# One hybrid block on one core: the opening in another order, and the plain gate and up blocks exchanged on the second half of the tokens

## The chip, the cores and the metric

The kernel runs on one core of a Trainium2 chip. The time is device microseconds of one launch; of several runs the median is shown. TensorE (PE in the profile) does the matrix products and the transposes, VectorE (DVE) and ScalarE (ACT) the elementwise work, SyncE (SP) issues most of the transfers, GpSimd (POOL) little. Each engine works through its own queue in order; semaphores hold an instruction until what it reads has been written, and until the room that it writes is free.

## The reference

One layer of a decoder block on 1024 tokens of width 1024, in float32:

```
h = rms_norm(x, attn_norm_w)
q, k, v, u, g = split(h @ w_in)            # 1024, 1024, 1024, 2048, 2048 columns
y_a = diff_attention(norm(q), norm(k), v) normed per head @ w_proj_attn
y_b = silu(layer_norm(conv31(u_a * sigmoid(u_b)))) @ w_proj_conv
x = x + (sigmoid(g_a) * y_a + sigmoid(g_b) * y_b) @ w_out
h = rms_norm(x, ffn_norm_w)
x = x + (silu(h @ W_gate) * (h @ W_up)) @ w_down          # FF = 2816 = 22 blocks of 128
```

## The kernel before, in words

**Products in three parts.** Every operand of a large product is split into a high part (a cast by ScalarE, `split_hi`, L120) and a low part (operand minus high part, VectorE, `split_lo`, L125). A product is three matmuls for each 128 of the contraction: high by high, high by low, low by high. So a tile is of use to TensorE only when ScalarE and then VectorE have been over it; a weight tile is 128x1024.

**The opening (`opening`, L817).** Tokens go in eight tiles of 128. For each: load (`xload`, two halves of 256 KB), sum of squares (`squares_of`, ScalarE), reciprocal root (`roots`: one VectorE instruction `v`, a root on ScalarE, five small VectorE instructions), scale by root and norm weight (`scale_x`, VectorE, two halves, reads `wb`, the norm weight broadcast to 128 partitions, called `anw_b` in the profile), transpose by TensorE in two halves (`turn_x`), and high and low part (`hi_x`, `lo_x`) into `hT_hi` and `hT_lo`. Beside it the first half of V is worked out, token tile by token tile: four weight pairs of 512 KB (`v_load`), cast by `w_hi(0..3)` and `w_lo(0..3)`, and 24 matmuls for each tile (`v_terms`). `TERMS` is the usual order, 8 steps of the contraction by three terms; in the first tile `halves` puts all terms with the high weights first. `v_out` splits the result and stores it. `w_hi(4)`, `w_lo(4)`, `w_hi(5)`, `w_lo(5)` are the two weight tiles of the first U block, loaded by `u_load` into the room of the first two V pairs (`wraw`, two buffers). After three V tiles the U block runs on token tiles 0 to 3 (`u_half`, L966) with the norm of tiles 4 to 7 between its matmuls.

**What sets the order.** A planner orders the program's instructions for each engine by a simulated time line. Inside `in_order(...)` (L199) the order of the code is kept on the engines named: in the three blocks of the opening TensorE, ScalarE, VectorE and SP. Each block ends with a `yield`, after which the loop at L996 may add taps of the convolution, once there are any. So in the opening the order in the code is the order on the engines, and what stands behind a waiting instruction waits too.

**The gate and up part.** Of the 22 blocks the first two (0 and 1) are done plainly, each on two halves of the tokens: `gate(f, sb, w)` is one GEMM of 24 matmuls and a silu, `up(f, sb, w, sg)` one GEMM and a product, stored to DRAM. `W[0]` and `W[1]` are the gate and up weights of block 0, `W[2]` and `W[3]` those of block 1. `W[0]` to `W[2]` lie in the three rotating buffers `whi`/`wlo`; `W[3]` (`fourth`, L538) lies in the room of the tile T4h. The second token half needs the norm of tiles 4 to 7 (`rest_of_rows`). The other 20 blocks go through a seven-product scheme (`pair`, L1661) which needs sums and differences of the token quarters: `differences()` (L1546) works out four differences per token tile in `xa` (16 VectorE operations) and splits them into T1 to T4 (16 casts, 16 low parts). It also needs sums of weight quarters, `s12` and `s34` in `prepare` (L1617; `s` in the profile), which lie in room that `xa` gives up. `prepare` takes the rotating buffers in turn: A11 and A12 come into the buffer of `W[0]`, the split of `s12` into that of `W[1]`, the split of `s34` into that of `W[2]`. `pair` starts with A11, A12, then S2 by T2 and S1 by T1.

Of the kernel before, what the change touches and what calls it, by code (L numbers as in the profile page):

```python
# [57 lines left out]
def kernel(  # L58
# [27 lines left out]
    nc = tc.nc  # L86
# [52 lines left out]
    def pg():  # L139
        npg[0] += 1  # L140
        p_, tag = pgs[npg[0] % len(pgs)]
        return p_.tile([P, 512], F32, tag=tag, name=nm("pg"))
# [48 lines left out]
    xload(0, 0)  # L191
    xload(0, 1, nc.scalar)
    for g in range(2):
        nc.scalar.dma_start(
            wb[:, 512 * g : 512 * (g + 1)], attn_norm_w[:, 512 * g : 512 * (g + 1)].to_broadcast([P, 512])
        )

# [505 lines left out]
    TERMS = [(k, a_, b_) for k in range(NKT) for a_, b_ in ((0, 0), (0, 1), (1, 0))]  # L703
# [113 lines left out]
    def opening():  # L817
# [11 lines left out]
        def u_load(z):  # L829
            c0 = (U0 + D, U0)[z]  # L830
            nc.sync.dma_start(
                uraw[z][:].rearrange("p (k c) -> p k c", c=P),
                win[:, c0 : c0 + P].rearrange("(k p) c -> p k c", p=P),
            )
# [8 lines left out]
        def w_hi(k):  # L843
            split_hi(tiles[k][0][:], raw6[k][:])

        def w_lo(k):
            split_lo(tiles[k][1][:], raw6[k][:], tiles[k][0][:])
# [3 lines left out]
        E_ = mybir.EngineType  # L851
        R, PT_ = {}, {}

        def turn_x(i, g):
            PT_[i, g] = x_turn(i, g)

        def hi_x(i, g):
            x_place(i, g, PT_[i, g], False)

        def lo_x(i, g):  # L860
            x_place(i, g, PT_[i, g], True)

        def squares_of(i, n):
            ss = sm.tile([P, 2], F32, tag="ss", name=nm("ss"))
            for e in range(n):
                x_squares(i + e, ss[:, e : e + 1])
            return ss

        def roots(i, n, ss):
            r = rstd_of(ss[:, :n], n, 1.0 / D)  # L870
            for e in range(n):
                R[i + e] = r[:, e : e + 1]

        def scale_x(i):
            for g in range(2):
                x_scale(i, R[i], g)

        with in_order(E_.PE, E_.Activation, E_.DVE, E_.SP):
            v_load(0)
            v_load(1)  # L880
            x_load(1)
            v_load(2)
            v_load(3)
            for i in range(2, NT):
                x_load(i)
            R[0] = x_first()
            scale_x(0)
            w_hi(0)
            turn_x(0, 0)
            hi_x(0, 0)  # L890
            turn_x(0, 1)
            lo_x(0, 0)
            w_hi(1)
            hi_x(0, 1)
            lo_x(0, 1)
            w_lo(0)
            ss = squares_of(1, 1)
            w_lo(1)
            u_load(0)
            u_load(1)  # L900
            roots(1, 1, ss)
            w_hi(2)
            scale_x(1)
            w_hi(3)
            w_lo(2)
            w_lo(3)
            o = pg()
            halves = [[(k, a_, 0) for a_ in range(2) for k in range(4 * g, 4 * g + 4)] for g in range(2)]
            v_terms(o, halves[0], w, 0, True, False)
            v_terms(o, halves[1], w, 0, False, False)  # L910
            v_terms(o, [(k, 0, 1) for k in range(4)], w, 0, False, False)
            turn_x(1, 0)
            hi_x(1, 0)
            lo_x(1, 0)
            turn_x(1, 1)
            ss = squares_of(2, 2)
            hi_x(1, 1)
            lo_x(1, 1)
            v_terms(o, [(k, 0, 1) for k in range(4, 8)], w, 0, False, True)
            roots(2, 2, ss)  # L920
            scale_x(2)
            v_out(0, 0, o)
        yield
        with in_order(E_.PE, E_.Activation, E_.DVE, E_.SP):
            o = pg()
            v_terms(o, TERMS[:12], w, 1, True, False)
            for g in range(2):
                turn_x(2, g)
                hi_x(2, g)
                lo_x(2, g)  # L930
            scale_x(3)
            w_hi(4)
            ss = squares_of(4, 2)
            v_terms(o, TERMS[12:], w, 1, False, True)
            roots(4, 2, ss)
            v_out(0, 1, o)
        yield
        with in_order(E_.PE, E_.Activation, E_.DVE, E_.SP):
            o = pg()
            v_terms(o, TERMS[:12], w, 2, True, False)  # L940
            for g in range(2):
                turn_x(3, g)
                hi_x(3, g)
                lo_x(3, g)
            w_lo(4)
            scale_x(4)
            w_hi(5)
            w_lo(5)
            ss = squares_of(6, 2)
            v_terms(o, TERMS[12:], w, 2, False, True)  # L950
            roots(6, 2, ss)
            scale_x(5)
            v_out(0, 2, o)
        yield

# [8 lines left out]
        sg = {}  # L964
# [581 lines left out]
    def differences():  # L1546
# [11 lines left out]
        for z in (2, 1, 3, 4):  # L1558
            for i in range(4):
# [2 lines left out]
                split_hi(T[z][0][:, :, ts], src)  # L1562
                split_lo(T[z][1][:, :, ts], src, T[z][0][:, :, ts])

    sg = gate(0, 1, W[0])
    up(0, 1, W[1], sg)
    differences()
    sg = gate(1, 1, W[2])
    up(1, 1, W[3], sg)
    n2_ctx.close()  # L1570
    xp_ctx.close()

# [229 lines left out]
```

## Time and profile before

| | before |
|---|---|
| three runs | 1762.86, 1764.28, 1766.6 us |
| median | 1764.28 us |
| the profiled execution, its own time | 1765.22 us |
| its span | 1763.4 us |
| TensorE busy | 1737.2 us (99%) |
| VectorE busy | 1272.2 us (72%) |
| ScalarE busy | 799.0 us (45%) |

The profile is of one execution. Times in its rows are microseconds from the start of the span. A row of the timeline gives start, length, engine, line of the program, operation, what is written and read, and, where the engine was idle before, for how long and who released it. In such names `px` is a transposed half token tile, `vwh`/`vwl` the V weights, `whi`/`wlo` other weights, `acc` and `pg` accumulators, `h_hi`/`h_lo` the second norm's result. Records of a matmul overlap: each lasts 0.39 us while the next starts 0.23 us behind it.

### The profile page before, as it was taken

How to read it: one execution, taken by the hardware profiler on the slowest of the kernel's cores; microseconds unless marked ns; L12 is line 12 of the kernel's file. 1: busy time of each engine (PE TensorE's matmuls, PEld its weight loads, DVE VectorE, ACT ScalarE, POOL GpSimd, SP SyncE). 2: the span in 40 equal slices, each digit the busy share in tenths (PEclk: the TensorE clock that was granted, in tenths of full speed). 3: DMA queues.
4: the chain of work that ended last, by engine and by line, in shares of the span. 5: the costliest groups of instructions: out<-in, count | busy, mean ns of one | idle time of the engine just before them, and what ended most of it. 6: DMA issues, size and time to landing. Idle time of an engine off the chain costs nothing.

```text
span 1763.4 us, 24974 instructions
## 1 busy us (share of the span) xinstructions
PE 1737.2 (99%) x8983; PEld 1481.3 (84%) x8983; DVE 1272.2 (72%) x2166; ACT 799.0 (45%) x1876; POOL 19.6 (1%) x92
## 2 busy tenths in 40 slices
PE   6999999999999999999999999999999999999999
PEld 5778898998989998988887888878888888888887
DVE  6598888998888888985877425867667666665544
ACT  5221141557767776764456213633333333333333
POOL 0000000000000000000000000000000000000000
PEclk9999999999999999999999999999999999999999
DMA  6337333235443344353863544224544544697663
GB/s 235 108 126 233 127 111 114 69 106 137 111 148 102 88 115 146 99 157 127 289 217 120 162 167 144 90 93 153 171 157 151 175 157 144 204 361 247 215 215 131
DMA packets 249814, 274.22 MB, mean 156 GB/s; under 512 B 16362, under 2 KB 165907, under 8 KB 249691
## 3 DMA queue, kind: packets, MB, share of 16 engines
q1 hardware_dynamic: 247834, 266.42, 46.9%
q0 software_dynamic: 1280, 4.91, 0.9%
q8 instruction: 70, 1.15, 0.3%
q10 hardware_dynamic: 576, 1.31, 0.2%
q14 instruction: 54, 0.43, 0.1%
HBM read 176.07 MB, written 78.16 MB: 144 GB/s over the span
## 4 chain that ended last, share of the span: by engine, by line
PE 90%; DMA 3%; DVE 3%; ACT 2%; issue 1%; SPq 0%; ACTq 0%; DVEq 0%
PE acc L1656 21%; PE pg L153 12%; PE pg L154 12%; PE pg L155 12%; PE acc L497 12%; PE pg L691 4%; PE sc L1056 2%; PE sc L1055 2%; PE pT L1091 2%; PE wo L153 2%; PE wo L155 2%; PE wo L154 2%; DMA ya_d<-gt 1%; PE pW L155 1%; DMA gt<-g_d 1%
## 5 line engine op out<-in xcount | busy, mean ns | idle before, releaser
L569 DVE SCALAR_TENSOR_TENSOR acc<-u,cw,acc 128x1024 f32<-128x1024 f32 x240 | 306.8, 1278 | 2.9
L153 PE MATMUL pg<-hT_hi,whi 128*128 128x512 f32 x512 | 201.8, 394 | 0.5 <-ACT sgg L601 0.2
L154 PE MATMUL pg<-hT_lo,whi 128*128 128x512 f32 x512 | 200.9, 392 | 0.0
L155 PE MATMUL pg<-hT_hi,wlo 128*128 128x512 f32 x512 | 200.7, 392 | 0.0
L125 DVE TENSOR_TENSOR wlo<-wraw,whi 128x1024 fp32r<-128x1024 f32 x101 | 123.1, 1219 | 83.4 <-ACT whi L120 79.3
L120 ACT CAST whi<-wraw 128x1024 fp32r<-128x1024 f32 x101 | 106.3, 1052 | 167.0 <-PE pg L154 89.9
L125 DVE TENSOR_TENSOR wlo<-draw,whi 128x1024 fp32r<-128x1024 f32 x75 | 91.8, 1224 | 90.2 <-ACT whi L120 84.9
L153 PE MATMUL pg<-whi,hT_hi 128*128 128x256 f32 x512 | 146.0, 285 | 0.5 <-ACT jk L759 0.5
L155 PE MATMUL pg<-whi,hT_lo 128*128 128x256 f32 x512 | 145.9, 285 | 0.0
L154 PE MATMUL pg<-wlo,hT_hi 128*128 128x256 f32 x512 | 145.5, 284 | 0.0
L120 ACT CAST whi<-draw 128x1024 fp32r<-128x1024 f32 x75 | 79.3, 1057 | 129.3 <-PE acc L497 125.8
L1062 ACT ACTIVATE E<-E,mn 128x256 f32<-128x256 f32 (+7 forms) x128 | 100.0, 783 | 46.7 <-DVE mn L1057 45.6
L497 PE MATMUL acc<-wlo,whi 128*128 128x512 f32 x308 | 119.8, 389 | 0.0
L497 PE MATMUL acc<-whi,wlo 128*128 128x512 f32 x308 | 119.8, 389 | 0.0
L153 PEld LDWEIGHTS pg<-hT_hi,whi 128*128 128x128 f32 x512 | 96.2, 188 | 20.6 <-ACT sgg L601 0.7
L155 PEld LDWEIGHTS pg<-hT_hi,wlo 128*128 128x128 f32 x512 | 96.2, 188 | 19.1
L154 PEld LDWEIGHTS pg<-hT_lo,whi 128*128 128x128 f32 x512 | 96.3, 188 | 19.0 <-issue 0.6
L153 PEld LDWEIGHTS pg<-whi,hT_hi 128*128 128x128 f32 x512 | 97.7, 191 | 2.3 <-ACT jk L759 1.1
L154 PEld LDWEIGHTS pg<-wlo,hT_hi 128*128 128x128 f32 x512 | 97.7, 191 | 1.3
L155 PEld LDWEIGHTS pg<-whi,hT_lo 128*128 128x128 f32 x512 | 97.7, 191 | 0.4
L1656 PE MATMUL acc<-h_hi,whi 128*128 128x512 f32 x240 | 93.4, 389 | 0.0
L1656 PE MATMUL acc<-h_lo,whi 128*128 128x512 f32 x240 | 93.4, 389 | 0.0
(284 smaller groups left out, 4185.8 us busy)
## 6 DMA issues: line engine op xcount, KB each, us to landing
wraw<-in_w_gate_up_dram SPq DMA_DIRECT2D x44, 512.0 KB, 4.7
wraw<-in_w_in_dram SPq DMA_DIRECT2D x38, 512.0 KB, 4.1
qs<-qs SPq DMA_DIRECT2D x96, 128.0 KB, 2.3
wd<-in_w_down_dram SPq DMA_DIRECT2D x44, 256.0 KB, 3.2
tdT<-wd SPq DMA_DIRECT2D x88, 128.0 KB, 4.7
draw<-sdS SPq DMA_DIRECT2D x44, 256.0 KB, 2.6
draw<-tdT SPq DMA_DIRECT2D x44, 256.0 KB, 3.0
wraw<-in_w_in_dram SPq DMA_DIRECT2D x32, 256.0 KB, 3.5
```

The lines of the kernel that those rows point to most:

```text
L120: act.copy(dst, src)
L125: last_lo[0] = dve.tensor_tensor(dst, src, f32(hi), op=ALU.subtract).ins
L153: pe.matmul(o, lh, rh, start=start, stop=False)
L154: pe.matmul(o, lh, rl, start=False, stop=False)
L155: last_mm[0] = pe.matmul(o, ll, rh, start=False, stop=stop).ins
L497: m = pe.matmul(o[s_][i][:], l_[:, ts], r_[:, 512:], start=start and j + y_ == 0, stop=j == n - 1 and y_ == 2, skip_group_check=not start,)
L569: dve.scalar_tensor_tensor(acc[0][:], us[c][:, t : t + S], cw[:, c, t : t + 1], acc[0][:], op0=ALU.mult, op1=ALU.add)
L691: last_mm[0] = pe.matmul(o[:], l_, r_, start=first and n_ == 0, stop=last and n_ == len(terms) - 1).ins
L1055: pe.matmul(o[:, :w], qh[:, qs], k, start=True, stop=False)
L1056: last_mm[0] = pe.matmul(o[:, :w], ql[:, qs], k, start=False, stop=True).ins
L1062: act.activation(e[:, :nk], e[:, :nk], AF.Exp, bias=mn[:, j : j + 1], scale=-1.0, accum_out=l[:, j : j + 1])
L1656: pe.matmul(o[:], a_[x_][:, k, :], b_[y_][:, k, :], start=start and k + x_ + y_ == 0, stop=k == 3 and x_ == 1, skip_group_check=not start,)
```

## The change

In the opening: the two loads of the norm weight go from ScalarE's queue to SP's, where they come ahead of the V weights. The first two blocks become one, in another order: two V weight casts ahead of the first `hi_x`; the low parts of the V weights spread out between the roots and scales; V tiles 0 and 1 side by side in two accumulators; the U loads behind `w_lo(2)`. In the third block `scale_x(4)` comes ahead of `w_lo(4)`, and `scale_x(5)` ahead of the last roots. In the plain gate and up part block 1 comes ahead of block 0 on the second half of the tokens. No operation is added or taken away.

```diff
     for g in range(2):
-        nc.scalar.dma_start(
+        nc.sync.dma_start(
             wb[:, 512 * g : 512 * (g + 1)], attn_norm_w[:, 512 * g : 512 * (g + 1)].to_broadcast([P, 512])
         )
...
             w_hi(0)
-            turn_x(0, 0)
-            hi_x(0, 0)
-            turn_x(0, 1)
-            lo_x(0, 0)
             w_hi(1)
-            hi_x(0, 1)
-            lo_x(0, 1)
+            for g in range(2):
+                turn_x(0, g)
+                hi_x(0, g)
+                lo_x(0, g)
             w_lo(0)
             ss = squares_of(1, 1)
+            roots(1, 1, ss)
+            w_hi(2)
+            w_hi(3)
+            scale_x(1)
             w_lo(1)
+            w_lo(2)
             u_load(0)
             u_load(1)
-            roots(1, 1, ss)
-            w_hi(2)
-            scale_x(1)
-            w_hi(3)
-            w_lo(2)
-            w_lo(3)
-            o = pg()
+            ss = squares_of(2, 2)
+            o, o1 = pg(), pg()
             halves = [[(k, a_, 0) for a_ in range(2) for k in range(4 * g, 4 * g + 4)] for g in range(2)]
+            lows = [[(k, 0, 1) for k in range(4 * g, 4 * g + 4)] for g in range(2)]
             v_terms(o, halves[0], w, 0, True, False)
             v_terms(o, halves[1], w, 0, False, False)
-            v_terms(o, [(k, 0, 1) for k in range(4)], w, 0, False, False)
-            turn_x(1, 0)
-            hi_x(1, 0)
-            lo_x(1, 0)
-            turn_x(1, 1)
-            ss = squares_of(2, 2)
-            hi_x(1, 1)
-            lo_x(1, 1)
-            v_terms(o, [(k, 0, 1) for k in range(4, 8)], w, 0, False, True)
+            for g in range(2):
+                turn_x(1, g)
+                hi_x(1, g)
+                lo_x(1, g)
+            w_lo(3)
             roots(2, 2, ss)
             scale_x(2)
-            v_out(0, 0, o)
-        yield
-        with in_order(E_.PE, E_.Activation, E_.DVE, E_.SP):
-            o = pg()
-            v_terms(o, TERMS[:12], w, 1, True, False)
+            v_terms(o, lows[0], w, 0, False, False)
+            v_terms(o1, halves[0] + halves[1], w, 1, True, False)
+            v_terms(o, lows[1], w, 0, False, True)
+            v_terms(o1, lows[0], w, 1, False, False)
             for g in range(2):
                 turn_x(2, g)
                 hi_x(2, g)
                 lo_x(2, g)
+            v_out(0, 0, o)
             scale_x(3)
+            ss = squares_of(4, 2)
+            v_terms(o1, lows[1], w, 1, False, True)
             w_hi(4)
-            ss = squares_of(4, 2)
-            v_terms(o, TERMS[12:], w, 1, False, True)
             roots(4, 2, ss)
-            v_out(0, 1, o)
+            v_out(0, 1, o1)
+        yield
         yield
...
+            scale_x(4)
             w_lo(4)
-            scale_x(4)
             w_hi(5)
             w_lo(5)
             ss = squares_of(6, 2)
             v_terms(o, TERMS[12:], w, 2, False, True)
+            scale_x(5)
             roots(6, 2, ss)
-            scale_x(5)
             v_out(0, 2, o)
...
+    sg = gate(1, 1, W[2])
+    up(1, 1, W[3], sg)
+    differences()
     sg = gate(0, 1, W[0])
     up(0, 1, W[1], sg)
-    differences()
-    sg = gate(1, 1, W[2])
-    up(1, 1, W[3], sg)
     n2_ctx.close()
     xp_ctx.close()
```

## The prediction

> **What bounds the kernel now.** I read the page first, then the table of TensorE's waits, then the timelines of the two places that the waits name.
>
> ```profile
> span 1763.4 us, 24974 instructions
> PE 1737.2 (99%) x8983; PEld 1481.3 (84%) x8983; DVE 1272.2 (72%) x2166; ACT 799.0 (45%) x1876; POOL 19.6 (1%) x92
> ```
> ```profile
> engine line waited for: us in total, times, longest us
> PE px L676 <- DVE xt L670: 11.5, 3, 8.6
> PE acc L1656 <- ACT whi L120: 2.4, 1, 2.4
> PE pg L691 <- ACT vwh L120: 2.1, 1, 2.1
> PE px L676 <- DVE hT_lo L125: 1.0, 1, 1.0
> ```
>
> TensorE (PE) is the bound: it is idle for 1763.4 − 1737.2 = 26 us only. The four waits hold 17 of them, and all lie where the diff works: three rows in the opening, one (L1656) at the seam between the plain gate and up blocks and the main loop. A change here is worth what it takes from TensorE's waits, plus what the clock loses behind them.
>
> **The seam (gate and up, block 1 first).** TensorE in order of time, and two stretches of it (of a stretch's last three figures the first is the granted clock):
>
> ```profile
> 1165.92 0.39 PE L1656 MATMUL acc<-h_hi,wlo 128*128 128x512 f32 x1
> ...
> 1170.00 0.39 PE L1656 MATMUL acc<-h_hi,wlo 128*128 128x512 f32 x1
> 1172.81 0.50 PE L1656 MATMUL acc<-T2h,whi 128*128 128x512 f32 x1 [2.42 <-ACT whi L120]
> ...
> 1180.25 0.39 PE L1656 MATMUL acc<-h_hi,whi 128*128 128x512 f32 x1
> ```
> ```profile
> 1170.40:1172.80 2.40, 0.00 (x0) 0.00 (x0) 2.40 (x6) 1.09 (x2) 0.00 (x0) 1.00 0.19 53
> ...
> 1174.00:1177.40 3.40, 3.35 (x9) 2.65 (x9) 2.37 (x3) 1.28 (x2) 0.00 (x0) 0.51 0.64 188
> ```
>
> From 1165.92 to 1170.00 a matmul starts every 4.08 / 18 = 0.2267 us. The next should start at 1170.23; the 24 that follow (all of T1 and T2) need 5.44 us, so the matmul of 1180.25 could have started at 1175.67. Lost: 4.58 us, of which 2.6 are the wait, 1.7 the half clock behind it (3.4 us at 0.51), the rest a short wait for `wlo`. ScalarE and VectorE show what is late:
>
> ```profile
> 1148.44 1.06 ACT L120 CAST whi<-wraw 128x1024 fp32r<-128x1024 f32 x1 [0.53 <-PE pg L154]
> ...
> 1166.12 2.19 ACT L120 CAST T4h<-xa 128x512 fp32r<-128x512 f32 x4 [5.52 <-PE pg L155]
> ...
> 1171.71 1.05 ACT L120 CAST whi<-s 128x1024 fp32r<-128x1024 f32 x1 [2.40 <-DVE s L1639]
> ```
> ```profile
> 1143.56 0.69 DVE L125 TENSOR_TENSOR h_lo<-tr,h_hi 128x512 fp32r<-128x512 f32 x1
> ...
> 1166.79 2.49 DVE L125 TENSOR_TENSOR T4l<-xa,T4h 128x512 fp32r<-128x512 f32 x4
> 1169.19 0.68 DVE L1638 TENSOR_TENSOR s<-wraw 128x512 f32<-128x512 f32 x1
> ...
> 1171.00 0.68 DVE L1639 TENSOR_TENSOR s<-s,wraw 128x512 f32<-128x512 f32 x1
> 1171.60 0.68 DVE L1670 TENSOR_TENSOR p<-acc,p 128x512 f32<-128x512 f32 x1
> ...
> 1172.80 1.22 DVE L125 TENSOR_TENSOR wlo<-s,whi 128x1024 fp32r<-128x1024 f32 x1
> ```
>
> The last `up` (1,1) reads `fourth`, the weight tile in T4h's room. So the T4 splits start at its end (1166.12), the sums `s` in the room of `xa` come behind them (1169.19), their cast at 1171.71, and the T2 product waits for that cast. With block 1 first nothing is added or removed: the same four GEMMs of 24 matmuls (5.44 us each) run in another order, and `up(1,1)` ends two GEMMs = 10.9 us earlier, near 1155. T4 and `s` then lie under `gate(0,1)` and `up(0,1)`, a stretch in which ScalarE stood idle before (5.52 us before 1166.12 alone). The stores of the four products change places on SP's queue only; they are read long after.
>
> What is late next: `W[0]` and `W[1]` are now released last. A11's cast (1148.44, when `gate(0,1)` ended) moves to about 1160, done with its low part 1.05 + 1.22 later, against a need at 1165.9. The cast of `s` goes into `W[1]`'s slot, free at about 1166.1: cast to 1167.2, low part to 1168.4. T2's first matmul comes after the 24 of A11 and A12, at 1165.9 + 5.44 = 1171.4. Margin 3 us, so I take the whole 4.58 less 0.2 for a matmul restart: **4.4 us**. Ends: 4.6 at the top; at the bottom 2, if the low part stays queued behind `p` of L1670 as at 1171.60, which waits for A12's end (1171.8): 0.6 + 1.2 us behind it, less what the high-part matmuls fill.
>
> **The opening.** VectorE, ScalarE, TensorE, and the windows of its idle stretches:
>
> ```profile
> 7.75 0.75 DVE L670 SCALAR_TENSOR_TENSOR xt<-xt,r,anw_b 128x512 f32<-128x512 f32 x1 [1.09 <-DMA anw_b<-in_attn_norm_w_dram]
> ...
> 9.59 0.75 DVE L670 SCALAR_TENSOR_TENSOR xt<-xt,r,anw_b 128x512 f32<-128x512 f32 x1 [1.08 <-DMA anw_b<-in_attn_norm_w_dram]
> ...
> 12.77 2.35 DVE L125 TENSOR_TENSOR vwl<-wraw,vwh 128x1024 fp32r<-128x1024 f32 x2
> ...
> 15.04 0.15 DVE L649 TENSOR_SCALAR v<-ss 128x1 f32<-128x1 f32 x1
> ...
> 16.42 1.41 DVE L670 SCALAR_TENSOR_TENSOR xt<-xt,r,anw_b 128x512 f32<-128x512 f32 x2
> ...
> 27.07 1.41 DVE L670 SCALAR_TENSOR_TENSOR xt<-xt,r,anw_b 128x512 f32<-128x512 f32 x2
> ...
> 37.05 1.22 DVE L125 TENSOR_TENSOR wlo<-wraw,whi 128x1024 fp32r<-128x1024 f32 x1
> ```
> ```profile
> 1.20 0.95 ACTq L194 DMA_DIRECT2D anw_b<-in_attn_norm_w_dram  x2
> ...
> 10.32 1.05 ACT L120 CAST vwh<-wraw 128x1024 fp32r<-128x1024 f32 x1
> ...
> 15.33 1.98 ACT L120 CAST vwh<-vraw 128x1024 fp32r<-128x1024 f32 x2
> ...
> 22.20 1.06 ACT L655 ACTIVATE xj<-xt 128x1024 bf16<-128x1024 f32 x1
> ```
> ```profile
> 21.08 1.04 PE L676 MATMUL px<-ident,xt 128*128 128x128 f32 x8
> ...
> 27.97 1.29 PE L676 MATMUL px<-ident,xt 128*128 128x128 f32 x8 [2.21 <-DVE xt L670]
> ...
> 38.68 0.39 PE L155 MATMUL pg<-hT_hi,wlo 128*128 128x512 f32 x1
> ...
> 45.74 1.25 PE L676 MATMUL px<-ident,xt 128*128 128x128 f32 x8 [0.98 <-DVE hT_lo L125]
> ```
> ```profile
> 14.30:16.40 2.10, 0.00 (x0) 0.00 (x0) 1.68 (x7) 1.18 (x3) 0.00 (x0) 1.00 1.05 405
> 16.40:20.10 3.70, 3.66 (x9) 2.46 (x10) 3.68 (x4) 0.91 (x1) 0.00 (x0) 0.55 1.05 404
> ...
> 25.80:27.90 2.10, 0.00 (x0) 0.00 (x0) 1.66 (x8) 0.68 (x2) 0.00 (x0) 1.00 0.17 53
> ```
>
> Prices from these rows: a 1024-wide cast 0.95 us from one to the next on ScalarE, its low part 1.13 on VectorE, a pair of scales 1.3, squares of one tile 1.15, from `v` to the scale it releases 1.4 (15.04 to 16.42).
>
> *`anw_b` from ScalarE's queue to SP's, ahead of the V weights.* The scales of tile 0 waited for it until 7.75 and 9.59; ahead of 1 MB of weights it should be there by 7.4, and the second scale is done near 8.1 instead of 10.3. Nothing is paid on ScalarE (it waits for x at that time). But `w_hi(0)` and `w_hi(1)` now stand ahead of the first `hi_x` in ScalarE's order, so what decides is the landing of the second V weight pair. The cast of 10.32 waited for nothing, so it was there by then; in the new order the same 2.1 MB (x tile 0, `anw_b`, two pairs) come first. I take 10.0; ends 9.5 (when the last of the 2.1 MB, `anw_b`, was there in the old run) and 11.2 (10.3 and 0.95 of issue time moved ahead of it on SP). The early `anw_b` is thus worth nothing by itself: `hi_x(0,0)` comes at 11.0 (it could have come at 8).
>
> The Trainium skill speaks against this edit: "DMA: Bandwidth & Descriptors", section "Issuing engines are not separate DMA queues", has it that queues of different engines share the same DMA engines, and that a second issuing engine saves only issue time. By it the move gives up 0.95 us of issue and lands the weights at 11.2, 1.2 us off the opening's gain; the trace shows the issue time (0.95) and not yet which holds.
>
> *`w_lo(1)` behind the roots, `w_lo` of pairs 2 and 3 behind the scale.* With `hi_x` at 11.0 and 11.5, `lo_x` at 11.6 and 12.2, `w_lo(0)` at 12.8, `v` of tile 1 comes at 13.9 (old 15.04, behind two low parts). `w_hi(2)` and `w_hi(3)` follow at 14.2 and 15.2 (old 15.33), tile 1 is scaled at 15.3 (old 16.42). TensorE's wait of 2.1 us before 16.40 shrinks to two of under 1 us; I take it that the half clock of 16.40 to 20.10 then goes too. The first 16 V matmuls end at 17.6, and tile 1 is turned at once, not behind low-part matmuls (old 21.08).
>
> *Two V tiles side by side.* `hi_x(1)` waits for the squares of tiles 2 and 3 until 18.4; `lo_x(1)` 19.1 and 19.7, `w_lo(3)` 20.3, `v` 21.4, scale of tile 2 at 22.8 (old 27.07, where TensorE stood 2.21 us). TensorE fills this with 28 matmuls of the two tiles (6.4 us), and turns tile 2 at 24.8 instead of 27.97: **3.2 us ahead**.
>
> *Scale 4 ahead of `w_lo(4)`.* TensorE now needs only 8.0 us from there to the U block (4 + 24 matmuls, two turns of 0.85), so it arrives at 32.8. The chain beside it is longer: `hi_x(2)` 25.4, `vh` 26.4, two squares 26.9, `w_hi(4)` 29.2, the root 30.2 (queued behind that cast), `vl` of tile 1 at 31.4, `lo_x(3)` 32.0, scale 4 33.2, `w_lo(4)` 34.5 to 35.7. The U block's third matmul needs that low part: 35.8 against 38.68, **2.9 us ahead**, after an idle stretch of some 2.5 us that the old run doesn't have (its `w_lo(4)` at 37.05 was just in time). Behind two of three such stretches here the clock was halved for 3.4 to 3.7 us (16.40 and 1174.00; not behind 25.80). I take it that it is, which costs 1.6 and leaves 1.3. The later wait for `hT_lo` (0.98 us before 45.74) goes, as TensorE then comes after it: **opening 2.2 us**. Without half clock 3.9. Bounds: 4.4 with the weights at 9.5 as well; a loss of 0.8 with the weights at 11.2, half clock until 20 and behind the new stall.
>
> The Trainium skill, "TensorE: Matmul & The Clock Gate", section "What's actually happening", puts the fall to half clock behind at least one idle window of about 3.4 us. By it the new 2.5 us would cost nothing more and the opening would give 3.9; the rows of 16.40 and 1174.00, half clock behind idle times of 2.1 and 2.4 us, go against it, and I follow the rows.
>
> *The rest.* The two U loads (512 KB each) are now issued behind `w_lo(2)`, in SP's order still behind all of x; their casts come at 29.2 at the earliest, and a load of that size was there 10.3 us into the span at the latest, beside all of the early traffic. The early stop between the first two V tiles moves behind both, where no taps are due yet: nothing. Scale 5 ahead of the last root is hidden by the U block's 12 matmuls (2.7 us) ahead of the turn that needs it.
>
> Nothing between the two places takes this back: TensorE is the bound there, and its transfers and taps are counted per step, not per time.
>
> **The sum.** 4.4 + 2.2 = 6.6 us. The profiled execution took 1765.22 us (its span and 1.8 around it): 1758.6 with the change. The median of the three runs is 0.9 lower, so by the median 1764.28 − 6.6 = **1757.7 us**.
>
> **Rivals.**
> - *No half clock behind the new stall*: 4.4 + 3.9, 1756.0. For it speaks the stretch of 25.80, against it the other two. 15%.
> - *The opening gives nothing*: weights at 11.2, half clock twice; the seam alone, 1759.9. For it: the chain of ScalarE and VectorE is as long as before from tile 2 on. 17%.
> - *The seam's wait only moves* to `wlo` of `s` behind `p`, with an idle time long enough for the half clock; the seam gives 1 us at most, the opening 2.2: 1761.5. For it the order 1171.60, 1172.80 of the old queue; against it that the cast of `s` ends 5 us sooner. 11%.
> - *Slower: the differences get ahead of the last norm.* In the old run the last `h_lo` (1143.56) was queued behind 13 of the 32 VectorE operations of `differences()`, and TensorE lost about half a microsecond at the start of the second-half GEMMs. T4 is free earlier now, so the planner may draw differences forward. Of the 19 left, 4 still wait for `up(1,1)`; each of 15 put ahead costs 0.60 us. From 9 of them (5.4, and 1.7 for the clock) the gain is gone; all 15 cost 10.7 against 6.6, so 1768.4. Against it: the GEMMs that need `h_lo` come just as soon as before. 6%.
>
> The forecast has the remaining 51%. A measurement of this kernel tells 0.2% (3.5 us) from no change. The forecast and the first two rivals are faster by more than that but for their tails (near the lower bound of the opening, or the bottom of the seam): 0.75. The third is the same, with those tails: 0.19. Slower 0.06. Range: 1755.0 (both gains near their tops) to 1762.4 (the third rival and a little more).
>
> **What would show it.** Right: no wait of T2's product for `whi`, T4 splits near 1154, no half clock in the stage behind; turn of tile 2 near 24.8, a wait of 2 to 3 us for `wlo` before the U block near 33 to 36, its third matmul near 35.8. Wrong: `hi_x(0,0)` later than 12 (weights late), half clock still at 17 to 20, a matmul wait for `wlo` or `T4l` at the seam, or VectorE differences ahead of the last `h_lo`.

## The result and the profile after

The changed kernel takes 1756.03 us (median of 6 runs, 1754.51 to 1758.6), the kernel before, run beside it, 1763.57 us (6 runs, 1760.62 to 1766.6): a ratio of 0.9958, interval 0.9947 to 0.9968, which is 5.6 to 9.3 us. The forecast was 1757.7 us and a gain of 6.6. A second series of the changed kernel gave 1756.43 us and 0.9955 (0.9942 to 0.9968).

The page of the changed kernel, its first lines, and three rows of the table of TensorE's waits (us in total, times, longest):

```profile
span 1754.1 us, 24980 instructions
PE 1735.0 (99%) x8983; PEld 1482.0 (84%) x8983; DVE 1273.5 (73%) x2166; ACT 796.0 (45%) x1876; POOL 19.5 (1%) x92
```
```profile
PE px L676 <- DVE xt L670: 7.5, 1, 7.5
PE pg L155 <- DVE wlo L125: 2.0, 1, 2.0
PE pg L691 <- ACT hT_hi L120: 1.6, 1, 1.6
```

TensorE's idle time went from 26 to 19 us. Of the four rows of before, the seam's (`acc` for `whi`) and that for `hT_lo` are gone, the first V matmul waits 1.6 us for `hT_hi` where a later one waited 2.1 for `vwh`, and the wait for `xt` has only its first one left, at the very start. New is the wait for `wlo` in front of the U block, which the prediction had at some 2.5 us.

**The seam.** ScalarE, VectorE and TensorE in order of time (start, length, and in brackets the idle time before and what ended it; lines are 4 lower than before):

```profile
1143.73 1.06 ACT L120 CAST whi<-wraw 128x1024 fp32r<-128x1024 f32 x1 [0.56 <-PE pg L154]
...
1149.40 2.18 ACT L120 CAST T4h<-xa 128x512 fp32r<-128x512 f32 x4 [2.57 <-PE pg L155]
...
1155.79 1.04 ACT L120 CAST whi<-s 128x1024 fp32r<-128x1024 f32 x1
```
```profile
1156.86 1.23 DVE L125 TENSOR_TENSOR wlo<-s,whi 128x1024 fp32r<-128x1024 f32 x1 [0.44 <-ACT whi L120]
```
```profile
1161.21 0.39 PE L1652 MATMUL acc<-h_hi,wlo 128*128 128x512 f32 x1
...
1165.52 0.39 PE L1652 MATMUL acc<-T1h,whi 128*128 128x512 f32 x1
...
1165.97 0.39 PE L1652 MATMUL acc<-T1h,wlo 128*128 128x512 f32 x1
...
1170.96 0.39 PE L1652 MATMUL acc<-h_hi,whi 128*128 128x512 f32 x1
```

The same stretch, the last 19 matmuls of A11 and A12 and the 24 of T1 and T2, now takes 1170.96 − 1161.21 = 9.75 us; before it was 1180.25 − 1165.92 = 14.33. The difference is 4.58 us, the whole of what the prediction had counted as lost. T1 now stands ahead of T2; both read halves of the same tile, the split of `s`. Its high part is there at 1156.8 and first read at 1165.52, its low part at 1158.1 and 1165.97.

**The opening.** The steps that carried the forecast, on ScalarE, VectorE and TensorE, and two windows (the last three figures are granted clock, share of the DMA engines, GB/s):

```profile
8.15 1.04 ACT L120 CAST vwh<-wraw 128x1024 fp32r<-128x1024 f32 x1 [2.55 <-DMA wraw<-in_w_in_dram]
9.48 1.04 ACT L120 CAST vwh<-wraw 128x1024 fp32r<-128x1024 f32 x1 [0.29 <-DMA wraw<-in_w_in_dram]
10.44 1.07 ACT L120 CAST hT_hi<-px 128x512 fp32r<-128x512 f32 x2
```
```profile
32.64 1.41 DVE L670 SCALAR_TENSOR_TENSOR xt<-xt,r,anw_b 128x512 f32<-128x512 f32 x2
33.97 2.35 DVE L125 TENSOR_TENSOR wlo<-wraw,whi 128x1024 fp32r<-128x1024 f32 x2
```
```profile
11.07 2.08 PE L691 MATMUL pg<-vwh,hT_hi 128*128 128x512 f32 x4 [1.63 <-ACT hT_hi L120]
12.94 1.91 PE L691 MATMUL pg<-vwh,hT_lo 128*128 128x512 f32 x4
...
17.22 1.03 PE L676 MATMUL px<-ident,xt 128*128 128x128 f32 x8
...
24.47 1.03 PE L676 MATMUL px<-ident,xt 128*128 128x128 f32 x8
...
35.24 0.50 PE L155 MATMUL pg<-hT_hi,wlo 128*128 128x512 f32 x1 [2.02 <-DVE wlo L125]
...
42.91 1.04 PE L676 MATMUL px<-ident,xt 128*128 128x128 f32 x8
```
```profile
32.87:36.28 3.41, 1.39 (x6) 0.86 (x5) 3.41 (x5) 1.66 (x4) 0.00 (x0) 1.00 0.20 73
36.28:39.70 3.42, 3.42 (x12) 2.73 (x11) 2.88 (x10) 1.42 (x3) 0.00 (x0) 0.50 0.94 274
```

Forecast and trace side by side: second V cast 10.0 and 9.48, turn of tile 1 17.6 and 17.22, turn of tile 2 24.8 and 24.47, idle stretch 2.5 and 2.02, third matmul of the U block 35.8 and 35.24, half clock behind it in both. Tile 5 is turned at 42.91 instead of 45.74, 2.8 us ahead.

**Where the 9.3 us of the two spans lie.** By the last turn of the opening the changed kernel is 3.0 us ahead, by the last turn of the second norm (some 1140 us in) 4.7, at the end 9.3: 3.0 + 1.7 + 4.6. The middle 1.7 can't be put down to the change: from behind the opening to the seam the instructions and the transfers stand in the same order on every engine in both kernels. The medians differ by 7.5.

### The profile page after: what moved, and what is told of

It reads as the page before. It is cut to its first block, busy times and chain, and to the rows that moved or that the text cites. A ratio compares the mean times of both kernels' runs of the same rounds, so it can differ in the third digit from the quotient of the medians.

```text
span 1754.1 us, 24980 instructions
## 1 busy us (share of the span) xinstructions
PE 1735.0 (99%) x8983; PEld 1482.0 (84%) x8983; DVE 1273.5 (73%) x2166; ACT 796.0 (45%) x1876; POOL 19.5 (1%) x92
## 4 chain that ended last, share of the span: by engine, by line
PE 94%; DMA 2%; ACT 2%; DVE 1%; SPq 0%; issue 0%; DVEq 0%
PE acc L1652 22%; PE pg L153 14%; PE pg L154 13%; PE pg L155 13%; PE acc L497 12%; PE pg L691 5%; PE sc L1052 2%; PE sc L1051 2%; PE wo L154 2%; PE pT L1087 2%; PE wo L153 2%; PE wo L155 2%; PE pW L155 1%; PE pW L153 1%; PE pW L154 1%; DMA vl<-v_lo 1%
```

## The experiments

In the table: the second V weight's cast, the turn of tile 5 (before: 45.74), how far the kernel is ahead of before's profile at the last turn of the opening, and the time from the last turn of the second norm to the end of the span (before: 623.7), which holds the seam. The last two columns are differences of times read to a tenth. "Seam alone" and so on are the runs told below.

| kernel | median (runs) | ratio to before | V cast | turn 5 | ahead | last stretch |
|---|---|---|---|---|---|---|
| the changed kernel | 1756.03 (6) | 0.9958 (0.9947 to 0.9968) | 9.48 | 42.91 | 3.0 | 619.1 |
| the same again | 1756.43 (5) | 0.9955 (0.9942 to 0.9968) | 10.17 | 43.52 | 2.5 | 619.7 |
| seam alone | 1759.59 (9) | 0.9978 (0.9968 to 0.9988) | – | – | −0.8 | 619.2 |
| opening alone | 1760.51 (11) | 0.9981 (0.9972 to 0.9990) | 10.70 | 43.63 | 2.1 | 622.3 |
| one GEMM of cover | 1760.31 (11) | 0.9979 (0.9970 to 0.9989) | – | – | −0.6 | 620.3 |
| 8 unread matmuls | 1757.06 (6) | 0.9958 (0.9946 to 0.9971) | 11.45 | 43.80 | 1.9 | 619.1 |
| 3 unread matmuls | 1755.70 (4) | 0.9953 (0.9936 to 0.9970) | 9.70 | 42.06 | 3.7 | 619.5 |
| low part ahead of scale 4 | 1757.24 (5) | 0.9956 (0.9944 to 0.9969) | 9.64 | 42.01 | 2.2 | 620.1 |
| U weight ahead of the squares | 1755.90 (6) | 0.9951 (0.9937 to 0.9964) | 9.92 | 41.16 | 4.6 | 619.1 |
| `anw_b` on ScalarE's queue | 1756.14 (5) | 0.9957 (0.9943 to 0.9972) | 10.52 | 43.88 | 2.1 | 619.2 |
| tile 0 ahead of the V casts | 1755.51 (5) | 0.9955 (0.9942 to 0.9968) | – | 43.10 | 2.9 | 619.2 |
| squares of 6, 7 late | 1753.87 (5) | 0.9945 (0.9931 to 0.9959) | 10.91 | 40.75 | 4.4 | 619.2 |
| both of the last two | 1755.78 (5) | 0.9956 (0.9942 to 0.9970) | – | 40.81 | 3.7 | 619.1 |

**Each half by itself.** Kernel before with the seam's order alone, and the changed kernel with the old order of the seam:

```diff
 # seam alone
+    sg = gate(1, 1, W[2])
+    up(1, 1, W[3], sg)
+    differences()
     sg = gate(0, 1, W[0])
     up(0, 1, W[1], sg)
-    differences()
-    sg = gate(1, 1, W[2])
-    up(1, 1, W[3], sg)
```

> The opening as before, gate and up block 1 ahead of block 0 on the second token half. If the late T4 splits and the sums s behind them make the seam's wait: TensorE's wait for whi (2.4 us) and the half clock behind it go, the T2 product follows A12 without a gap, 4.4 to 4.6 us faster than the kernel before, with the turn of token tile 5 still near 45.7 us. If the gain at the seam needs the new opening, or the planner moves the wait elsewhere: less than 1.5 us.

> The new opening, the gate and up order as before. Theory: 2.8 to 3.0 us ahead at the turn of token tile 5 (near 42.9 us instead of 45.74), the wait of 2.4 us for whi at the seam as before, and 2.8 to 3.0 us faster in all. The 1.7 us that the changed kernel gained besides, between 760 and 1110 us, where no engine's order differs: if it is the scatter of transfer times from run to run, it doesn't come back with this opening in particular; if it belongs to the new opening, this kernel is 4.5 us faster and is further ahead at 1100 us than at 100 us.

The seam alone gives 0.0022 x 1763 = 3.9 us (2.1 to 5.6), the opening alone 3.3 us (1.8 to 4.9); the sum, 7.2, agrees with the 7.5 of both. The seam's stretch of 43 matmuls takes 9.74 us in the profile of the seam alone. With the opening alone the seam's wait stands as before, and so does the new wait for `wlo`, here without half clock behind either:

```profile
37.03 0.50 PE L155 MATMUL pg<-hT_hi,wlo 128*128 128x512 f32 x1 [2.02 <-DVE wlo L125]
...
43.63 1.26 PE L676 MATMUL px<-ident,xt 128*128 128x128 f32 x8 [0.42 <-DVE hT_lo L125]
...
1165.61 0.39 PE L1652 MATMUL acc<-h_hi,wlo 128*128 128x512 f32 x1
...
1172.50 0.50 PE L1652 MATMUL acc<-T2h,whi 128*128 128x512 f32 x1 [2.42 <-ACT whi L120]
...
1178.45 0.39 PE L1652 MATMUL acc<-h_hi,whi 128*128 128x512 f32 x1
```

So its last stretch is 1.4 us shorter than before's although the seam's order is the same: that is the seam's half clock, missing in this execution. The stretch of 43 matmuls takes 1178.45 − 1165.61 = 12.84 us, between the 14.33 of before and the 9.75 of the changed kernel: the wait alone loses 3.1 us, the half clock 1.5 more where it comes. A wait of 2.4 us in the same place brings the half clock in one execution and not in the other, and so does one of 2.02 in front of the U block. That is taken up below. Of the 1.7 us in the middle this kernel shows nothing: 2.1 us ahead at the end of the opening, it is 0.3 ahead at the last turn of the second norm.

**How much cover the seam needs.** Before with only `gate(1,1)` and `up(1,1)` drawn ahead of `up(0,1)`: one GEMM in place of two lies behind them.

```diff
+    sg0 = gate(0, 1, W[0])
     sg = gate(1, 1, W[2])
     up(1, 1, W[3], sg)
     differences()
-    sg = gate(0, 1, W[0])
-    up(0, 1, W[1], sg)
+    up(0, 1, W[1], sg0)
```

> The opening as before; second token half in the order gate 0, gate 1, up 1, differences, up 0: up 1 ends one GEMM (5.45 us) earlier than before instead of two. If what counts is that T4 and s are over before T2 is due: T4 starts near 1160.7, the low part of s ends near 1168.6, T2 is due near 1171.4, so the whole 4.4 to 4.6 us are gained as with two GEMMs. If the gain goes with the length of the cover: about half, 2.3 us.

There is no wait for `whi` or `wlo` left, and the seam's stretch takes 9.75 us, as with both GEMMs. The one wait behind it is another, some 365 us later (at 1529.09):

```profile
PE acc L1656 <- DVE u L1684: 0.9, 1, 0.9
```

The last stretch is 3.4 us shorter than before's, against 4.6 with both GEMMs; 0.9 of the difference is that wait. The times of the two don't tell them apart (the intervals overlap over most of their length). One GEMM is thus enough for the wait that was removed, as a margin of 7.9 us less 5.4 lets one expect.

**The changed kernel again, with the new idle time filled, and with the low part ahead of scale 4.** The three ran beside each other.

```diff
 # 8 unread matmuls between the second and the third U matmul
+            for n in range(8):
+                pe.matmul(o[:], hT_hi[:, 0, 0:P], w[0][0][:, 0, :], start=n == 0, stop=n == 7)
 # low part ahead of scale 4
-            scale_x(4)
             w_lo(4)
+            scale_x(4)
```

> The changed kernel once more, beside the three variants of this call: 0.9958 of the time before, 7.5 us, as measured; turn of token tile 5 near 42.9 us; what it gains between 760 and 1110 us shows whether the 1.7 us found there come back.

> The changed kernel with eight matmuls on finished data, whose result nobody reads, between the second and the third matmul of the first U product, where TensorE waits 2.0 us for wlo. No wait gets shorter: the third matmul stays near 35.2 us. If the idle time is what halves the clock behind it: no half clock from 36.3 to 39.5 us, the turn of token tile 5 near 41.3 instead of 42.9 us, 1.6 us faster than the changed kernel. If the clock falls for another reason: no difference.

> The changed kernel with w_lo(4) ahead of scale_x(4) again, as before the change. Theory: the third matmul of the first U product comes 1.3 us earlier, near 33.9 us, behind an idle time of under 1 us, so the clock stays whole: 2.4 to 2.9 us faster than the changed kernel. If the half clock comes all the same: 1.3 us. If scale_x(4) then is late for the turn of tile 4: nothing.

The second series of the changed kernel repeats the first, but its V weights are cast at 8.83 and 10.17, 0.7 us later, and everything behind them is later by as much: third U matmul less second V cast is 25.76 there and 25.75 here, in line with the forecast's 35.8 − 10.0. The half clock is there again (36.10 to 39.52), and so is the gain in the middle, 2.2 us (2.5 ahead behind the opening, 4.7 at the second norm). The eight matmuls (their result is read by nothing) took the half clock away. By the time alone they gave nothing, since in this execution the weights came at 11.45; counted from the cast, the turn of tile 5 came at 32.35 instead of 33.43, 1.1 us sooner, and then waited 0.44 us for `hT_lo`.

```profile
37.18 0.50 PE L378 MATMUL pg<-hT_hi,wlo 128*128 128x512 f32 x1 [0.21 <-DVE wlo L125]
...
43.80 1.25 PE L682 MATMUL px<-ident,xt 128*128 128x128 f32 x8 [0.44 <-DVE hT_lo L125]
```

With the low part ahead of scale 4 the wait for `wlo` shrank to 0.70 us, and another appeared behind it: the turn of tile 5 waited 1.80 us for `hT_lo` (42.01), and now the half clock fell behind that one.

```profile
42.01 1.36 PE L676 MATMUL px<-ident,xt 128*128 128x128 f32 x8 [1.80 <-DVE hT_lo L125]
```
```profile
39.61:43.02 3.41, 1.61 (x12) 1.01 (x10) 3.27 (x10) 2.76 (x5) 0.00 (x0) 1.00 0.80 249
43.02:46.44 3.42, 3.42 (x11) 2.74 (x9) 3.37 (x6) 0.85 (x2) 0.00 (x0) 0.50 0.16 59
```

The turn of tile 5 is 1.1 us sooner, counted from the cast, but the half clock behind it takes that back, and the 2.4 to 2.9 us that were expected don't appear. So the order of scale 4 and `w_lo(4)` moves the stall from one place to the next; it doesn't remove it.

**The first U weight ahead of the squares of tiles 4 and 5.**

```diff
             scale_x(3)
+            w_hi(4)
+            w_lo(4)
             ss = squares_of(4, 2)
             v_terms(o1, lows[1], w, 1, False, True)
-            w_hi(4)
             roots(4, 2, ss)
...
             scale_x(4)
-            w_lo(4)
```

> The changed kernel with w_hi(4) and w_lo(4) moved into the block ahead, behind scale_x(3) and ahead of the squares of tiles 4 and 5. Theory: w_lo(4) ends near 30 us, before TensorE needs it at 33; no idle time and no half clock there: the turn of token tile 5 near 39.7 us, 3.0 to 3.5 us faster than the changed kernel. If the roots of tiles 4 and 5, now later, hold up lo_x(3) or scale_x(4) in turn: under 1.5 us.

```profile
41.16 1.25 PE L676 MATMUL px<-ident,xt 128*128 128x128 f32 x8 [1.56 <-DVE hT_lo L125]
```

The wait for `wlo` is gone and the turn of tile 5 comes 31.24 us behind the cast (33.43 in the changed kernel), after 1.56 us for `hT_lo`, without half clock; that is 41.16 and not the 39.7 expected. The opening is 4.6 us ahead of before. The time, 1755.90, is lower than the changed kernel's but not by more than the intervals allow, and not by the 3 us expected.

**The next limit.** The same kernel with the squares and roots of tiles 6 and 7 behind the turns of tile 4, since they stood ahead of `hi_x(4)` on ScalarE; and with tile 0's turn, `hi_x` and `lo_x` ahead of the first two V casts, by itself and together with that.

```diff
 # squares of 6, 7 late
-            ss = squares_of(6, 2)
             v_terms(o, TERMS[12:], w, 2, False, True)
             scale_x(5)
-            roots(6, 2, ss)
             v_out(0, 2, o)
...
+            if nxt == 6:
+                roots(6, 2, squares_of(6, 2))
             if nxt is not None:
                 scale_x(nxt)
 # tile 0 ahead of the V casts
-            w_hi(0)
-            w_hi(1)
             for g in range(2):
                 turn_x(0, g)
                 hi_x(0, g)
                 lo_x(0, g)
+            w_hi(0)
+            w_hi(1)
```

> The kernel with w_hi(4) and w_lo(4) ahead of the squares of tiles 4 and 5, and besides the squares and roots of tiles 6 and 7 moved behind the turns of tile 4 (they stood ahead of hi_x(4) on ScalarE). Theory A (the next limit behind the U block's wait is the chain squares, roots, hi_x(4), lo_x(4), which TensorE waited 1.56 us for before the turn of tile 5): that wait goes, the turn of tile 5 comes near 39.5 (41.2 without this move, 42.9 in after), and the time is 1754.0 to 1755.0. Rival B (the low parts of U's weights on VectorE, or the landing of the next weights, hold it): the wait for hT_lo stays at 1 us or more or another one follows at the turns of tiles 6 and 7, and the time stays at 1755.9.

> After, with turn, hi_x and lo_x of tile 0 ahead of the casts of the first two V weights on ScalarE. Theory A (in after everything behind is queued behind the second V weight's cast, so the opening shifts one to one with the landing of that weight): hi_x of tile 0 near 8.5 whatever the weights do; the first V matmul still needs the weights, so it starts near 11 (second cast + 1); only the late-landing runs gain. Third U matmul minus second cast shrinks from 25.7 to 24.5 to 25; time 1755.0 to 1756.5. Rival B (the chain from tile 2 on sets it, squares and low parts, not the first cast): third U matmul stays near 35.2, time as after.

> The same kernel as the run with the squares of tiles 6 and 7 late, and turn, hi_x, lo_x of tile 0 also ahead of the first two V weight casts. Theory A (gains of the opening add while TensorE is the bound from there on): 0 to 1 us below that run, 1753.2 to 1755.0; the turn of tile 5 near 39. Rival B (no gain, since the first V matmul needs both): the same time and the same turn of tile 5 relative to the second V weight's cast.

With the squares late the wait of 1.56 us becomes 0.22, and the turn of tile 5 comes 29.84 us behind the cast; at 40.75 it is later than the 39.5 expected, since the weights came a microsecond late (10.91). What now stands ahead of `hi_x(4)` on ScalarE is the cast of the next U weight, which waits for its transfer:

```profile
37.15 1.05 ACT L120 CAST whi<-wraw 128x1024 fp32r<-128x1024 f32 x1 [2.36 <-DMA wraw<-in_w_in_dram]
38.10 1.07 ACT L120 CAST hT_hi<-px 128x512 fp32r<-128x512 f32 x2
```
```profile
40.75 1.25 PE L676 MATMUL px<-ident,xt 128*128 128x128 f32 x8 [0.22 <-DVE hT_lo L125]
```

At 1753.87 us (1752.2 to 1754.93) this is the lowest time of the study, 2.2 below the changed kernel. Only one of its five runs is above the lowest run of the changed kernel, though the intervals of the two ratios overlap.

Tile 0 ahead of the casts gave nothing: `hi_x(0,0)` came at 8.48, but `hi_x(0,1)` only at 9.60, behind a slow turn (its 8 transposes took 2.21 us, against 1.03 later on), so the V casts began at 10.08 and the first V matmul at 11.18 (11.07 in the changed kernel). Counted from the second cast (11.03) the third U matmul came sooner, 24.43 us instead of 25.76, but the cast came later by more (9.48 there): the third U matmul stands at 35.46, as the rival expected.

```profile
8.48 0.59 ACT L120 CAST hT_hi<-px 128x512 fp32r<-128x512 f32 x1 [3.08 <-PE px L676]
9.60 0.59 ACT L120 CAST hT_hi<-px 128x512 fp32r<-128x512 f32 x1 [0.53 <-PE px L676]
10.08 1.99 ACT L120 CAST vwh<-wraw 128x1024 fp32r<-128x1024 f32 x2
```

Together with the late squares it gave no gain either: there the next U weight's cast came at 37.84, behind a wait of 1.48 us for its transfer, and the turn of tile 5 waited 1.52 us again. So what is left in this stretch seems to depend on when U's weights land; no run changed that by itself.

**`anw_b` back on ScalarE's queue.**

```diff
-        nc.sync.dma_start(
+        nc.scalar.dma_start(
             wb[:, 512 * g : 512 * (g + 1)], attn_norm_w[:, 512 * g : 512 * (g + 1)].to_broadcast([P, 512])
```

> After, with the two loads of anw_b back on ScalarE's queue, so that the V weights are issued two steps earlier on SP's. Theory A (the landing of the V weights sets the opening, whichever queue issues anw_b): the casts of the first two V weights come at 8 to 9.5 as in after, but the scale of tile 0 is done only near 10.3, hi_x near 11.5, the third U matmul 0.5 to 1 us later than in after; time 1756.5 to 1757.5. Rival B (each issue ahead of the weights on SP delays them by 0.9 us): the casts come near 7, the chain behind is bound by the scale alone, and the third U matmul comes no later than in after; time 1756 or less. Either way the difference to after lies near what the interval can tell, so the places of the third U matmul and of the first V matmul decide, not the time.

```profile
7.91 1.05 ACT L120 CAST vwh<-wraw 128x1024 fp32r<-128x1024 f32 x1 [2.30 <-DMA wraw<-in_w_in_dram]
10.52 1.04 ACT L120 CAST vwh<-wraw 128x1024 fp32r<-128x1024 f32 x1 [1.56 <-DMA wraw<-in_w_in_dram]
```

The first weight is there at 7.9, as in the kernel before, the second at 10.5, inside the 9.48 to 11.45 that it has with the other order. Third U matmul at 36.25, turn of tile 5 at 43.88, both a microsecond later than in the first profile of the changed kernel and within 0.4 of the second; time the same. So neither expectation is met in full. The first weight, at 8.15 to 10.12 with the other order, comes earlier; for the second, one profile against a spread of 2 us shows no shift, and the second is the one that counts.

**Which idle time brings the half clock.** The windows above show half clock from 36.28 to 39.70 and from 43.02 to 46.44: 3.42 us each, beginning 1.0 us after the matmuls had started again. In the other profiles with half clock here it lasts as long too, beginning 0.2 to 1.4 us behind the restart. In all 14 traces the changes of the clock lie whole multiples of 3.413 us apart. So the clock seems to be set for windows of that length on a grid of its own. Counted on from the edges of the stretches, such windows can be laid through a whole profile. The kernel before and, counted on from the first entry of the clock in its trace (18.28, about where its matmuls reach full speed), the opening alone:

```profile
13.38:16.79 3.41, 1.28 (x6) 0.67 (x4) 2.97 (x9) 1.57 (x3) 0.00 (x0) 1.00 1.06 408
16.79:20.20 3.41, 3.38 (x9) 2.26 (x8) 3.31 (x4) 0.52 (x1) 0.00 (x0) 0.50 1.04 399
23.62:27.03 3.41, 2.14 (x10) 1.45 (x8) 1.58 (x7) 2.07 (x5) 0.00 (x0) 1.00 0.49 149
27.03:30.44 3.41, 2.43 (x14) 2.04 (x15) 3.21 (x6) 1.73 (x3) 0.00 (x0) 1.00 0.37 127
1170.50:1173.91 3.41, 1.10 (x4) 0.67 (x4) 3.41 (x5) 2.20 (x3) 0.00 (x0) 1.00 0.45 127
1173.91:1177.32 3.41, 3.36 (x9) 2.57 (x9) 2.38 (x3) 1.37 (x2) 0.00 (x0) 0.50 0.67 196
```
```profile
31.93:35.34 3.41, 3.09 (x14) 2.22 (x12) 3.27 (x10) 3.38 (x7) 0.00 (x0) 1.00 0.47 175
35.34:38.75 3.41, 1.72 (x7) 1.42 (x8) 3.41 (x5) 1.02 (x2) 0.00 (x0) 1.00 0.13 37
...
1168.57:1171.98 3.41, 1.50 (x7) 0.93 (x5) 3.41 (x7) 1.00 (x2) 0.00 (x0) 1.00 0.48 157
```

The first figure behind the length is TensorE's busy time. Behind windows with 1.10, 1.28, 1.39 and 1.61 us the next window is at half clock; behind 1.50, 1.72, 2.14 and 2.43 it isn't. The wait at 25.80 in the kernel before was as long as the one at 14.30, but the edge at 27.03 cuts it into two. The bound lies near 1.5 to 1.6 us; that 1.50 and 1.61 stand the wrong way round says how sharp such a reading is, the ends of matmuls being modelled. Over all 14 traces, from the first entry of the clock on, it holds but for that pair: behind each of the 22 windows with at most 1.46 us the clock is halved, and of those with 1.50 or more only behind the one with 1.61. This was read after the runs; a run made on it uses three unread matmuls instead of eight, which leaves 1.34 us idle:

```diff
-            for n in range(8):
+            for n in range(3):
```

> After, with 3 unread matmuls (in place of the 8 of the earlier run; their result is read by nothing) between the second and the third U matmul, so that the idle time there is 2.02 - 3 x 0.2267 = 1.34 us. Theory A (the clock is set window by window on a grid of 3.413 us that runs by itself, and is halved in the window behind one in which TensorE was busy for less than about 1.5 of the 3.41 us): at most 1.34 us are idle in any window, so no half clock behind it, in whatever phase the grid stands; the turn of tile 5 comes 32.4 us behind the second V weight's cast (33.4 in after), with a short wait for hT_lo; time 1755.5 to 1757. Rival B (an idle stretch of any size near 1 to 2 us may bring the half clock, by chance): half clock for 3.41 us behind it as in four of the five runs with an idle stretch of 2 us here, and the turn of tile 5 stays 33.4 behind the cast.

```profile
35.42 0.50 PE L378 MATMUL pg<-hT_hi,wlo 128*128 128x512 f32 x1 [1.34 <-DVE wlo L125]
...
42.06 1.25 PE L682 MATMUL px<-ident,xt 128*128 128x128 f32 x8 [0.46 <-DVE hT_lo L125]
```
```profile
36.00:40.00 4.00, 4.00 (x23) 3.40 (x22) 3.33 (x10) 1.58 (x3) 0.00 (x0) 1.00 0.89 256
```

Full clock behind it, and the turn of tile 5 comes 42.06 − 9.70 = 32.36 us behind the cast, as expected (32.4). On this run's grid all of the idle time lies in the window 32.31 to 35.72, with 2.07 us busy; without the three matmuls it would have been some 1.39. So it isn't an edge that saved the clock here. It is one execution, so it bears the reading out rather than proves it.

## Why the prediction was right, and where not

**The seam, 4.4 us: right, and shown.** The stretch became 4.58 us shorter, and takes 9.74 or 9.75 us in all twelve profiles with the new order or with half of it; the seam alone gives 3.9 us (2.1 to 5.6) by the times. The prediction took the half clock behind the wait as always there. With the opening alone it wasn't, and then the seam costs 3.1 us instead of 4.6, so the mean gain should lie between the two. The T4 splits do start where `up(1,1)` ends: 1149.40, in a run that is 4.7 us ahead there, so near 1154 on the old scale, as said. Wrong in detail was the step on the buffers: "A11's cast moves to about 1160" and "the cast of `s` goes into `W[1]`'s slot, free at about 1166.1". Here the buffers were taken in the order in which they were released. A11's cast came at 1143.73, right behind `gate(1,1)` in the buffer that it gave up, and the cast of `s` at 1155.79, when `gate(0,1)` had ended. The 1171.4 for T2's first matmul was wrong too: the prediction's own rows have 19 matmuls in front of it, not 24, and so 1170.23, which leaves 1.8 us of its margin of 3. What was there is 7.9 us (1158.1 to 1165.97). The term stayed right because a margin that is there isn't paid for. The rival with the wait merely moved to `wlo` fails on that margin. The slower rival fails too: where the second-half GEMMs begin, the changed kernel is 4.7 us ahead, just as at the last turn of the second norm, and in both kernels the same 13 of the 32 operations of `differences()` stand ahead of the last `h_lo` on VectorE.

**The opening, 2.2 us: right, a little small.** Each step came within 0.6 us of its forecast. It is 3.0 and 2.5 us ahead in the two profiles of the changed kernel, 2.1 with the opening alone. The term that decides is the landing of the second V weight, as said ("what decides is the landing of the second V weight pair"). It was taken as 10.0 and measured at 9.48, 10.17, 10.70 and, in kernels alike up to there, at 9.64 to 11.45. All that follows moves with it (the third U matmul comes 25.72 to 25.76 us behind it in five profiles with this order, 26.33 in that of the opening alone), so part of the scatter between executions of this kernel may be that of one transfer; how much, the times don't tell. The bounds 9.5 and 11.2 were about right.

**The half clock behind the new idle time: taken, and there,** though not always. It costs 7.67 us from the third U matmul to the turn of tile 5 (35.24 to 42.91) against 6.64 with three unread matmuls (35.42 to 42.06), so 1.0 net; 0.46 of the 1.5 that it costs by itself would otherwise be spent waiting for `hT_lo`. The prediction had 1.6 and nothing behind it. The rival without half clock, 1756.0 us, is the measured median but for 0.03, and the time alone would have spoken for it. The trace speaks against it: the half clock was there in both profiles of the changed kernel. Of the 1.7 us by which the median lies below the forecast, 0.7 are luck, as the kernel before took 1763.57 us beside it and not 1764.28; the rest is about what the two places gave beyond their terms (0.2 and 0.3 to 0.8). The Trainium skill, "TensorE: Matmul & The Clock Gate", section "What's actually happening", has the clock set by windows of 3.4 us that run freely, and has it fall after an idle window. The trace agrees with the first (36.28 to 39.70, starting 1.0 us behind the restart) and not with an idle window having to be whole: 1.39 of 3.41 us were busy.

**`anw_b` on SP's queue, taken at nothing:** not contradicted, 1756.14 against 1756.43 and 1756.03 us. The loss of 1.2 us that the prediction worked out for it, by way of the 0.95 us of issue time, is smaller than the intervals (some 2.5 us to each side) can tell. In the trace it does not appear: with the old queue the second cast is at 10.52, not earlier, and with the new one between 9.48 and 11.45 in eight profiles. The Trainium skill, "DMA: Bandwidth & Descriptors", section "Issuing engines are not separate DMA queues", has it that another issuing engine saves no more than the time to issue. The run doesn't go against it; what it doesn't bear out is the step from there to a later landing of the second weight.

**"The opening gives nothing" and "half clock twice"** fell with the opening alone, 3.3 us (1.8 to 4.9). One step of the opening was right only in its effect: the half clock of 16.40 to 20.10 is indeed gone, but the first V matmuls run at half speed in every kernel. Four of them take 12.94 − 11.07 = 1.87 us, 0.47 each, and in the changed kernel's profile full speed (0.23) comes only at about 16, though the clock column reads 1.00 throughout. The forecast of 17.6 for the turn of tile 1 names two waits of under 1 us and no half clock; there were one wait of 1.63 us and nearly 5 us at half speed. That it held all the same is in part luck.

**The sum.** 4.4 + 2.2 was forecast, 4.6 + 3.0 is in the profile, 7.5 (5.6 to 9.3) in the times. Nothing in between gave anything back. But nothing in between is steady either: with the seam alone, whose order on the computing engines is that of the kernel before up to the seam, the profile is 0.8 us behind at the end of the opening and 3.0 ahead at the last turn of the second norm, and with the opening alone 1.8 us are lost between the two. So a difference of 1 to 2 us between single profiles, away from the place of an edit, carries no cause with it; the places near the edit do. What makes up this scatter in the middle stays open.

## What to carry to other kernels

Where TensorE is at 99%, look for its few waits, count the time that they take and the half clock behind them, and see which room or which queue makes the late tile late: here an exchange of two blocks with no other cost gave 4.6 us in the trace. An order changed on two other engines only moves a stall until the whole chain behind it is shorter, so work out the next wait too (`wlo`, then `hT_lo`, then a transfer). For a gain of a microsecond measure places in the trace relative to the transfer that everything hangs on, since the time of a run doesn't show it.

## What the runs showed of the hardware that was not expected

- The half clock comes in stretches of 3.41 to 3.42 us on a grid of its own, behind a window of that length in which TensorE was busy for less than some 1.5 to 1.6 us (always at 1.46 or less, once at 1.61, never else). An idle stretch of about 2 us cost 1.5 us more where it lay in one window, and nothing more where an edge cut it. A few unread matmuls that leave 1.34 us idle kept the full clock.
- The same transfer of 512 KB at the start, behind the same other transfers, landed up to 2 us apart from execution to execution (cast at 9.48 to 11.45 us, in eight profiles).
- At the start of the span the clock column reads 1.00 while matmuls are 0.47 us apart: there the spacing tells the clock, not the column.
